# Latent attention: rotated query halves projected for eight heads at a time and passed through a DRAM scratch, both rotations ahead of all scores

## The chip, the cores and the metric

One Trainium2 chip, one core. The metric is the device time of one execution in microseconds (us), of which lower is better. Below, TensorE is the matrix engine, VectorE, ScalarE and GpSimd are the three engines for elementwise work, and SyncE issues nearly all DMAs. In the profile they are PE, DVE, ACT, POOL and SP.

## The reference

Two decoder layers over 512 tokens of width 1024, all in f32. Layer 0 mixes tokens with multi-head latent attention, layer 1 with a sparse attention; each layer then attends to 256 memory tokens and runs a gated feed-forward network, and a LayerNorm follows every part. The change lies in layer 0's latent attention alone:

```python
h = x @ w_in                                   # 512 + 256 + 32 columns
q = rms_norm(c_q) @ w_uq                       # 16 heads x (64 plain + 32 rotary)
q = concat(q[:64], rope(q[64:], pos))          # x1*cos - x2*sin, x1*sin + x2*cos
kv = rms_norm(c_kv) @ w_ukv                    # 16 heads x (64 key + 64 value)
k = concat(k_nope, rope(k_rope, pos))          # one 32-wide rotary key for all heads
p = softmax(mask(q @ k.T / sqrt(96)))          # causal, 512 x 512 per head
out = concat_heads(p @ v) @ w_o
```

## The kernel before

Every f32 operand of a matmul is split in two fp32r tiles, a high part `h` and the rest `l` (`split`, L94: ScalarE casts, VectorE or, if asked, GpSimd subtracts). `mm3` (L115) then makes one product out of three matmuls, h*h, h*l and l*h. `chunk` (L103) loads 512 KB of weights into one of three `raw` buffers through SyncE's queue and splits them into `wh` and `wl`, of which there are five each.

Tokens are the moving side, 512 columns at once. After the compressed projections (L465 to L545) come, in the order of the program, sixteen heads in pairs. `mla_proj(h)` (L565) projects the query of one head: 128 rows of output, which are 64 plain and 32 rotary rows, and the 32 rotary rows again with their halves swapped. A table multiplies them (`T0` for an even head, `T1` for an odd one: ones on the plain rows, cosine and signed sine on the others, L584), and the result is split. The key tile `K8` holds 64 plain key rows and the rotated key twice, so the sum over 128 rows of the product makes both terms of the rotation. At an even head it also projects the keys of the pair (6 matmuls) and loads the next weights. `mla_scores(h)` (L589) makes four score tiles of 128 queries and their softmax; `mla_t` (L603) transposes the probabilities, `mla_pv` (L624) multiplies them with the values, and at every odd head normalises and splits the output of the pair; `mla_v` (L516) projects values five steps ahead. The loop at L655 has `mla_t(h)`, `mla_scores(h + 1)`, `mla_proj(h + 3)`, `mla_pv(h)` and `mla_v(h + 5)`.

In the same loop `bias_rows` (L258) writes, head by head, a table of layer 1 to DRAM. The address ranges of two neighbouring rows overlap, so that each is issued when the one before has landed.

A planner orders each engine's instructions at compile time from the order of the program, a model of durations, and the buffers that are free; on the chip each engine then runs its list strictly in order and waits on semaphores. PSUM has four banks for projections, transposes and products with V (tag a) and four for scores and values (tag b). There are 39 tiles of 128x512 (`t2`) for nearly all that moves.

Of the kernel before, what the change touches and what calls it, by code (L numbers as in the profile page):

```python
# [11 lines left out]
F32 = mybir.dt.float32  # L12
FR = mybir.dt.float32r
# [7 lines left out]
P = 128  # L21
# [26 lines left out]
def _constants():  # L48
    c = np.zeros((P, 8), np.float32)
    r = np.arange(P)  # L50
    c[:, 0] = np.array(INV_FREQ, np.float32)[r % 16]
    sw = (r >= 64) & (r % 32 < 16)
    c[sw, 0] *= -1.0
    c[:64, 1] = 0.25
    c[:64, 2] = np.pi / 2
    lo = np.array(BUCKET_LO, np.float32)
    hi = np.concatenate([lo[1:], [np.float32(3e38)]])
    lo[0] = -3e38
    c[:, 3] = lo[r % 32]
# [7 lines left out]
def tile_hybrid_mla_dsa_deepnorm_block(ctx: ExitStack, tc: tile.TileContext, A: dict, out: bass.AP):  # L67
# [360 lines left out]
    def trig():  # L428
        posf, ang, kk = t2(), t2(), t2()
        nc.vector.tensor_copy(posf, posi)  # L430
        nc.vector.tensor_scalar(ang, posf, cst[:, 0:1], None, op0=ALU.mult)
        two_pi = 2 * math.pi
        pieces = []
        rest = two_pi
        for _ in range(2):
            e = math.frexp(rest)[1]
            q = math.ldexp(math.floor(math.ldexp(rest, 11 - e)), e - 11)
            pieces.append(q)
            rest -= q
        pieces.append(rest)  # L440
        MAGIC = 1.5 * 2.0 ** 23
        for sh in (20, 10, 0):
            s = 2.0 ** sh
            if sh:
                nc.vector.tensor_scalar(kk, ang, 1.0 / (two_pi * s), MAGIC, op0=ALU.mult, op1=ALU.add)
            else:
                nc.vector.tensor_scalar(kk, ang, 1.0 / two_pi, cst[:, 1:2], op0=ALU.mult, op1=ALU.add)
                nc.vector.tensor_scalar(kk, kk, MAGIC, None, op0=ALU.add)
            nc.vector.tensor_scalar(kk, kk, MAGIC, None, op0=ALU.subtract)
            for q in pieces:  # L450
                nc.vector.scalar_tensor_tensor(ang, kk, -q * s, ang, op0=ALU.mult, op1=ALU.add)
            yield
        nc.vector.tensor_scalar(ang, ang, cst[:, 2:3], math.pi, op0=ALU.add, op1=ALU.min)
        nc.vector.tensor_scalar(ang, ang, -math.pi, None, op0=ALU.max)
        nc.scalar.activation(TK, ang, AF.Sin)
        nc.vector.tensor_copy(T0[64:96], TK[0:32])
        nc.scalar.copy(T0[96:128], TK[64:96])
        nc.vector.tensor_copy(T1[0:32], TK[0:32])
        nc.scalar.copy(T1[32:64], TK[64:96])
        yield  # L460

    TK, T0, T1 = t2(), t2(), t2()
    nc.gpsimd.memset(T0[0:64], 1.0)
    nc.gpsimd.memset(T1[64:128], 1.0)
    ps2 = [bank("b") for _ in range(NT)]  # L465
    for c in range(4):
        h, l = XT[c // 2]
# [78 lines left out]

    ka = t2()
    kb_ = t2()
    nc.vector.tensor_tensor(ka[0:64], pk[0:64], TK[0:64], op=ALU.mult)
    nc.vector.tensor_tensor(kb_[0:64], pk[64:128], TK[64:128], op=ALU.mult)  # L550
    nc.vector.tensor_tensor(ka[0:64], ka[0:64], kb_[0:64], op=ALU.add)
    K8 = [t8(), t8()]
    for i, k8 in enumerate(K8):
# [8 lines left out]

    OTs = []

    def mla_proj(h):  # L565
        pr, e = h // 2, h % 2
        if e == 0:
            wts["q"] = chunk(A["w_uq"][pr], (P, 4, 256), nc.gpsimd if pr > 1 else None)
            if pr % 4 == 0:
                wts["k"] = chunk(A["w_uk"][pr // 4], (P, 2, 512))  # L570
            wk = wts["k"]
            pkk = bank("a")
            c0 = P * (pr % 4)
            for k in range(2):
                mm3(pkk, (wk[0][:, k, c0:c0 + P], wk[1][:, k, c0:c0 + P]), (ckv[0][:, k], ckv[1][:, k]), k == 0, k == 1)
            k8 = K8[pr % 2]
            split(k8[0:64, 0], k8[0:64, 1], pkk[0:64])
            split(k8[64:128, 2], k8[64:128, 3], pkk[64:128])
        wq = wts["q"]
        pq = bank("a")  # L580
        for k in range(4):
            mm3(pq, (wq[0][:, k, P * e:P * e + P], wq[1][:, k, P * e:P * e + P]), (cq[0][:, k], cq[1][:, k]), k == 0, k == 3)
        tq = t2()
        nc.vector.tensor_tensor(tq, pq, (T0, T1)[e], op=ALU.mult)  # L584
        q = (t2(FR), t2(FR))
        split(q[0], q[1], tq)
        return q

    def mla_scores(h, q):  # L589
        e = h % 2  # L590
        k8 = K8[h // 2 % 2]
        s01 = t2()
        sx = Softmax([s01[:, 0:128], s01[:, 128:384], t2()[:, 0:384], t2()])
        for qt in range(NT):
            n = P * (qt + 1)
            N = max(n, 256)
            ps = bank("b")
            ts_ = slice(P * qt, P * qt + P)
            mm3(ps[:, :N], (q[0][:, ts_], q[1][:, ts_]), (k8[:, 2 * e, :N], k8[:, 2 * e + 1, :N]), True, True)
            sx.exp(qt, ps[:, :n], MSC, mask[:, 512 - n:512])  # L600
        return sx

# [21 lines left out]
    def mla_pv(h, PT):  # L624
# [12 lines left out]
        if e == 1:  # L637
            pr_ = bank("a")
            for qt in range(NT):
                nc.tensor.transpose(pr_[:, P * qt:P * qt + P], rb[:, qt].rearrange("p a b -> p (a b)"), ident)  # L640
            nc.vector.tensor_tensor(of, of, pr_, op=ALU.mult)
            if pr < 4:
                oh_, ol_ = OT8[0][:, pr], OT8[1][:, pr]
            else:
                oh_, ol_ = t2(FR), t2(FR)
            OTs.append((oh_, ol_))
            split(oh_, ol_, of)

# [454 lines left out]
def layout(inputs):  # L1103
# [15 lines left out]
    cols = []  # L1119
    for h in range(16):  # L1120
        nope, rope = uq[:, h, :64], uq[:, h, 64:]
        rs = [rope, rope[:, 16:], rope[:, :16]]
        cols += [nope] + rs if h % 2 == 0 else rs + [nope]
    uq = np.concatenate(cols, 1)
    f["w_uq"] = uq.reshape(4, P, 8, 256).transpose(2, 1, 0, 3).reshape(8, P, 1024)
# [40 lines left out]
```

## Time and profile before

| | us |
|---|---|
| median of 3 runs (lowest, highest) | 1559.26 (1556.68, 1560.79) |
| the profiled execution | 1561.3 |
| its span, first to last instruction | 1559.5 |

One execution was profiled on the chip; all numbers are microseconds unless marked ns. A matmul's recorded duration overlaps the next one's, so the pace of a row of matmuls is read from their starts. PEld is the load of weights into TensorE. The latent attention's heads lie between about 56 and 216 us of the span.

### The profile page before, as it was taken

To read this page: it belongs to the slowest core of one execution; us is meant where nothing else is said; L and a number is where in the kernel's file an instruction comes from. 1 tells how busy PE (TensorE), PEld (TensorE's weight loads), DVE (VectorE), ACT (ScalarE), POOL (GpSimd) and SP (SyncE) were. 2 spreads that over 40 slices of the span, in tenths; PEclk is the share of its full clock that TensorE was granted. 3 is DMA by queue.
4 is the path that set the end of the run, shared out by engine and by line. 5 is a ranking of instruction groups with operands and counts; after the bars stand their busy time and mean duration, and the time that the engine had idled before them with its cause. 6 is when DMAs were issued, how large, how long until landed. Compare 5 with 4: busy or idle time off the path is not lost.

```text
span 1559.5 us, 20796 instructions
## 1 busy us (share of the span) xinstructions
PE 1513.7 (97%) x7948; PEld 1290.8 (83%) x7948; DVE 998.4 (64%) x1706; ACT 659.1 (42%) x1182; POOL 306.8 (20%) x303
## 2 busy tenths in 40 slices
PE   8999999999999999999999789999999999999997
PEld 7788778988888888888788678889888888888886
DVE  5887868454746565654668968785448466556545
ACT  4676753343233333332246489434332333333230
POOL 1322101000132331400125522010001323324002
PEclk9999999999999999999999899999999999999999
DMA  6234323322323232223241236243223132322221
GB/s 219 71 103 115 131 87 122 124 93 95 122 96 107 79 120 90 100 88 110 80 149 68 88 122 236 72 143 111 95 95 134 70 122 72 118 95 95 95 95 54
DMA packets 51320, 166.79 MB, mean 107 GB/s; under 512 B 5300, under 2 KB 11748, under 8 KB 49172
## 3 DMA queue, kind: packets, MB, share of 16 engines
q1 hardware_dynamic: 50788, 164.41, 30.8%
q8 instruction: 62, 1.02, 0.3%
q10 hardware_dynamic: 432, 1.05, 0.2%
q14 instruction: 38, 0.31, 0.1%
HBM read 161.20 MB, written 9.47 MB: 109 GB/s over the span
## 4 chain that ended last, share of the span: by engine, by line
PE 78%; DMA 8%; DVE 7%; ACT 4%; issue 1%; POOL 1%; SPq 0%; POOLq 0%; ACTq 0%; DVEq 0%
PE ps L118 24%; PE ps L116 24%; PE ps L117 24%; DMA scr<-vscr 4%; DVE t L96 2%; DVE wl L96 1%; ACT wh L95 1%; DMA raw<-in_mla_o_dram 1%; ACT t L95 1%; ACT t L405 1%; PE ps L324 1%; DVE t L954 1%; POOL sm L267 1%; PE ps L1022 1%; DVE m L953 1%
## 5 line engine op out<-in xcount | busy, mean ns | idle before, releaser
L116 PE MATMUL ps<-t,wh 128*128 128x512 f32 (+1 forms) x1264 | 459.1, 363 | 3.5 <-DVE t L96 3.4
L117 PE MATMUL ps<-t,wh 128*128 128x512 f32 (+1 forms) x1264 | 458.2, 362 | 0.9 <-DVE t L96 0.9
L118 PE MATMUL ps<-t,wl 128*128 128x512 f32 (+1 forms) x1264 | 458.1, 362 | 0.0
L95 ACT CAST wh<-raw 128x1024 fp32r<-128x1024 f32 (+2 forms) x218 | 227.4, 1044 | 470.5 <-PE ps L117 163.3
L96 DVE TENSOR_TENSOR wl<-raw,wh 128x1024 fp32r<-128x1024 f32 (+2 forms) x202 | 260.9, 1293 | 227.7 <-ACT wh L95 225.9
L116 PE MATMUL ps<-wh,t 128*128 128x512 f32 (+2 forms) x838 | 304.9, 364 | 3.8 <-DVE t L96 1.5
L118 PE MATMUL ps<-wh,t 128*128 128x512 f32 (+2 forms) x838 | 303.1, 362 | 1.0 <-DVE t L96 1.0
L117 PE MATMUL ps<-wl,t 128*128 128x512 f32 (+2 forms) x838 | 302.0, 360 | 0.0
L116 PEld LDWEIGHTS ps<-t,wh 128*128 128x128 f32 x1264 | 238.6, 189 | 41.6 <-DVE t L96 5.2
L117 PEld LDWEIGHTS ps<-t,wh 128*128 128x128 f32 x1264 | 238.6, 189 | 37.9 <-DVE t L96 1.4
L118 PEld LDWEIGHTS ps<-t,wl 128*128 128x128 f32 x1264 | 238.6, 189 | 36.7
L116 PEld LDWEIGHTS ps<-wh,t 128*128 128x128 f32 x838 | 158.8, 189 | 27.5 <-ACT t L95 1.8
L118 PEld LDWEIGHTS ps<-wh,t 128*128 128x128 f32 x838 | 158.8, 190 | 24.7 <-DVE t L96 1.4
L117 PEld LDWEIGHTS ps<-wl,t 128*128 128x128 f32 x838 | 158.9, 190 | 23.0
L95 ACT CAST t<-ps 128x512 fp32r<-128x512 f32 (+2 forms) x241 | 118.5, 523 | 132.2 <-PE ps L324 87.6
L265 POOL TENSOR_SCALAR sm<-sm 128x1 f32<-128x1 f32 x32 | 19.5, 608 | 678.9 <-DVE sm L299 635.9
L96 DVE TENSOR_TENSOR t<-ps,t 128x512 fp32r<-128x512 f32 (+2 forms) x241 | 138.7, 603 | 20.4 <-ACT t L95 19.6
L95 ACT CAST wh<-t 128x1024 fp32r<-128x1024 f32 x56 | 58.9, 1052 | 141.6 <-PE ps L117 123.6
L96 DVE TENSOR_TENSOR wl<-t,wh 128x1024 fp32r<-128x1024 f32 x56 | 71.2, 1272 | 64.9 <-ACT wh L95 63.1
L832 DVE TENSOR_TENSOR t<-ps,t 128x512 f32<-128x512 f32 x44 | 30.4, 691 | 120.4 <-PE ps L118 120.4
L96 DVE TENSOR_TENSOR t<-t,t 128x512 fp32r<-128x512 f32 (+2 forms) x113 | 84.0, 746 | 24.3 <-ACT t L95 22.1
L95 ACT CAST t<-t 128x512 fp32r<-128x512 f32 (+3 forms) x137 | 70.5, 525 | 59.6 <-POOL t L766 33.5
(176 smaller groups left out, 1687.5 us busy)
## 6 DMA issues: line engine op xcount, KB each, us to landing
raw<-in_ffn_in_dram SPq DMA_DIRECT2D x88, 512.0 KB, 3.2
t<-in_ffn_dg_dram SPq DMA_DIRECT2D x16, 1024.0 KB, 5.0
raw<-in_xa_k_dram SPq DMA_DIRECT2D x16, 512.0 KB, 3.3
raw<-in_xa_v_dram SPq DMA_DIRECT2D x16, 512.0 KB, 3.8
raw<-in_xa_q_dram SPq DMA_DIRECT2D x16, 512.0 KB, 3.9
raw<-in_xa_o_dram SPq DMA_DIRECT2D x16, 512.0 KB, 3.2
raw<-in_ffn_dl_dram SPq DMA_DIRECT2D x12, 512.0 KB, 3.2
scr<-vscr SPq DMA_DIRECT2D x16, 319.5 KB, 4.2
```

Of the source, the lines that this page charges most:

```text
L95: nc.scalar.copy(h, src)
L96: (eng or nc.vector).tensor_tensor(l, src, h.bitcast(F32), op=ALU.subtract)
L116: nc.tensor.matmul(ps, st[0], mv[0], start=start, stop=False, skip_group_check=more)
L117: nc.tensor.matmul(ps, st[0], mv[1], start=False, stop=False, skip_group_check=more)
L118: nc.tensor.matmul(ps, st[1], mv[0], start=False, stop=stop, skip_group_check=more)
L265: nc.gpsimd.tensor_scalar(a, var, scale, eps, op0=ALU.mult, op1=ALU.add)
L267: nc.gpsimd.tensor_tensor(b, a, mhalf, op=ALU.pow)
L324: nc.tensor.transpose(pt[:, k], x_of(tt)[:, 512 * n + P * k:512 * n + P * k + P], ident)
L405: nc.scalar.activation(Sx, src, AF.Exp, bias=nb, scale=scale, accum_out=self.sm[:, i:i + 1])
L832: nc.vector.tensor_tensor(sg, pu, sg, op=ALU.mult)
L953: nc.vector.max(out=m8, in_=acc[:, :n])
L954: nc.vector.match_replace(out=acc[:, :n], in_to_replace=m8, in_values=acc[:, :n], imm_value=-3e38)
```

## The change

The columns of the query weights are put in another order: first the rotary columns, 128 first halves and 128 second halves for eight heads, twice, then the plain columns of two heads at a time. `mla_rope(o)` projects the rotary halves of eight heads, rotates them with four multiplications and one subtraction and addition, splits the two results, and writes the four tiles to a DRAM scratch `rsc`, which is laid out by group, head, and high and low halves. `mla_nope(pr)` projects the plain halves of a pair and splits them. For each head it makes one stationary tile: GpSimd copies the 64 plain high rows, and a DMA reads the head's 64 rotary rows (high and low) from the scratch into the other 64. A second tile, `zq`, holds the plain low rows and zeros; three such pairs are kept, and their zeros are written once. `mla_k(pr)` is the key projection by itself. The scores still take three matmuls, the third now with `zq`. The cosine and sine tables are whole tiles. The split of a pair's output goes from VectorE to GpSimd.

Both calls of `mla_rope`, two of `mla_k` and two of `mla_nope` stand ahead of the first scores. In the loop `mla_k` comes at odd heads and `mla_nope` at even ones.

```diff
+    rsc = dp.tile([2, 8, 4, 16, S], F32, name="rsc")
...
-        nc.scalar.activation(TK, ang, AF.Sin)
-        nc.vector.tensor_copy(T0[64:96], TK[0:32])
-        nc.scalar.copy(T0[96:128], TK[64:96])
-        nc.vector.tensor_copy(T1[0:32], TK[0:32])
-        nc.scalar.copy(T1[32:64], TK[64:96])
+        for e in range(2):
+            nc.scalar.activation(COS[64 * e:64 * e + 64], ang[0:64], AF.Sin)
+            nc.scalar.activation(SIN[64 * e:64 * e + 64], ang[64:128], AF.Sin)
...
-    def mla_proj(h):
-        pr, e = h // 2, h % 2
-        if e == 0:
-            wts["q"] = chunk(A["w_uq"][pr], (P, 4, 256), nc.gpsimd if pr > 1 else None)
...
-        for k in range(4):
-            mm3(pq, (wq[0][:, k, P * e:P * e + P], wq[1][:, k, P * e:P * e + P]), (cq[0][:, k], cq[1][:, k]), k == 0, k == 3)
-        tq = t2()
-        nc.vector.tensor_tensor(tq, pq, (T0, T1)[e], op=ALU.mult)
-        q = (t2(FR), t2(FR))
-        split(q[0], q[1], tq)
-        return q
+    def q_block(w, c0):
+        ps = bank("a")
+        for k in range(4):
+            mm3(ps, (w[0][:, k, c0:c0 + P], w[1][:, k, c0:c0 + P]), (cq[0][:, k], cq[1][:, k]), k == 0, k == 3)
+        return ps
+
+    def mla_rope(o, eng):
+        w = chunk(A["w_uq"][o], (P, 4, 256))
+        x1, x2 = q_block(w, 0), q_block(w, P)
+        r1, r2, t1, t2_ = t2(), t2(), t2(), t2()
+        nc.vector.tensor_tensor(r1, x1, COS, op=ALU.mult)
+        nc.vector.tensor_tensor(r2, x1, SIN, op=ALU.mult)
+        nc.vector.tensor_tensor(t1, x2, SIN, op=ALU.mult)
+        nc.vector.tensor_tensor(t2_, x2, COS, op=ALU.mult)
+        eng.tensor_tensor(r1, r1, t1, op=ALU.subtract)
+        eng.tensor_tensor(r2, r2, t2_, op=ALU.add)
+        for i, r_ in enumerate((r1, r2)):
+            h_, l_ = t2(FR), t2(FR)
+            split(h_, l_, r_, eng)
+            nc.sync.dma_start(rsc[o, :, i], h_.bitcast(F32))
+            nc.sync.dma_start(rsc[o, :, 2 + i], l_.bitcast(F32))
+
+    def mla_nope(pr):
+        if pr % 2 == 0:
+            wts["q"] = chunk(A["w_uq"][2 + pr // 2], (P, 4, 256), nc.gpsimd if pr else None)
+        ps = q_block(wts["q"], P * (pr % 2))
+        qh, ql = t2(FR), t2(FR)
+        split(qh, ql, ps)
+        qa, qz = [], zq[pr % 3]
+        for e in range(2):
+            q = t2(FR)
+            rows, other = slice(64 * e, 64 * e + 64), slice(64 - 64 * e, 128 - 64 * e)
+            nc.gpsimd.tensor_copy(q[rows], qh[rows].bitcast(F32))
+            nc.gpsimd.tensor_copy(qz[e][rows], ql[rows].bitcast(F32))
+            nc.sync.dma_start(q[other].bitcast(F32), rsc[pr // 4, (2 * pr + e) % 8].rearrange("s i t -> (s i) t"))
+            qa.append(q)
+        qs[pr] = qa, qz
...
-            mm3(ps[:, :N], (q[0][:, ts_], q[1][:, ts_]), (k8[:, 2 * e, :N], k8[:, 2 * e + 1, :N]), True, True)
+            nc.tensor.matmul(ps[:, :N], qa[e][:, ts_], k8[:, 2 * e, :N], start=True, stop=False)
+            nc.tensor.matmul(ps[:, :N], qa[e][:, ts_], k8[:, 2 * e + 1, :N], start=False, stop=False)
+            nc.tensor.matmul(ps[:, :N], qz[e][:, ts_], k8[:, 2 * e, :N], start=False, stop=True)
...
-            split(oh_, ol_, of)
+            split(oh_, ol_, of, nc.gpsimd)
...
-    qs = {0: mla_proj(0), 1: mla_proj(1)}
-    Ss = {0: mla_scores(0, qs[0])}
-    qs[2] = mla_proj(2)
+    mla_rope(0, nc.vector)
+    mla_k(0)
+    mla_nope(0)
+    mla_nope(1)
+    mla_k(1)
+    mla_rope(1, nc.gpsimd)
+    Ss = {0: mla_scores(0)}
     for h in range(16):
         PT = mla_t(h, Ss.pop(h))
         if h + 1 < 16:
-            Ss[h + 1] = mla_scores(h + 1, qs[h + 1])
-        if h + 3 < 16:
-            qs[h + 3] = mla_proj(h + 3)
+            Ss[h + 1] = mla_scores(h + 1)
+        if h % 2 and h // 2 + 2 < 8:
+            mla_k(h // 2 + 2)
+        if h % 2 == 0 and 1 < h // 2 + 1 < 8:
+            mla_nope(h // 2 + 1)
         mla_pv(h, PT)
```

## Rows read from the trace of the kernel before

**Rows 1.** The page: busy time of each engine, and two lines in 40 slices.
```profile
PE 1513.7 (97%) x7948; PEld 1290.8 (83%) x7948; DVE 998.4 (64%) x1706; ACT 659.1 (42%) x1182; POOL 306.8 (20%) x303
...
PE   8999999999999999999999789999999999999997
...
PEclk9999999999999999999999899999999999999999
```

**Rows 2.** Busy time by stretch: opening, loop over heads, end of the loop.
```profile
core 0: us, PE busy (x) PEld busy (x) DVE busy (x) ACT busy (x) POOL busy (x), PEclk, DMA share, GB/s
56.00:72.00 16.00, 14.74 (x72) 11.66 (x71) 13.41 (x24) 9.52 (x20) 7.21 (x4) 1.00 0.30 108
72.00:182.00 110.00, 105.63 (x618) 90.36 (x616) 90.55 (x229) 80.50 (x205) 20.59 (x40) 1.00 0.31 88
182.00:216.00 34.00, 28.48 (x169) 23.87 (x169) 25.20 (x63) 21.46 (x55) 2.72 (x12) 1.00 0.37 137
```

**Rows 3.** Timeline of TensorE in the opening: start, duration, instruction.
```profile
56.71 0.48 PE L116 MATMUL ps<-t,wh 128*128 128x512 f32 x1
...
60.31 0.39 PE L116 MATMUL ps<-t,wh 128*128 128x512 f32 x1
...
64.85 0.39 PE L116 MATMUL ps<-t,wh 128*128 128x512 f32 x1
65.31 0.38 PE L116 MATMUL ps<-t,t 128*128 128x256 f32 x1
...
71.74 0.71 PE L613 MATMUL ps<-ident,t 128*128 128x128 f32 x5
```

**Rows 4.** Groups by form, 56 to 216 us: busy us, mean ns | idle before.
```profile
L96 DVE TENSOR_TENSOR t<-t,t 128x512 fp32r<-128x512 f32 x23 | 19.8, 860 | 5.0 <-ACT t L95 4.9
...
L95 ACT CAST t<-t 128x512 fp32r<-128x512 f32 x23 | 14.2, 616 | 10.9 <-DVE t L584 7.5 <-DVE t L641 3.1 <-DVE sm L409 0.3
...
L96 DVE TENSOR_TENSOR t<-ps,t 128x512 fp32r<-128x512 f32 x17 | 11.6, 681 | 1.6 <-ACT t L95 1.6
...
L584 DVE TENSOR_TENSOR t<-ps,t 128x512 f32<-128x512 f32 x16 | 11.1, 691 | 9.3 <-PE ps L118 9.2
...
L96 DVE TENSOR_TENSOR wl<-raw,wh 128x1024 fp32r<-128x1024 f32 x7 | 8.6, 1221 | 4.6 <-ACT wh L95 4.6
```

**Rows 5.** GpSimd's groups, 0 to 216 us: split of weights, two copies of keys.
```profile
L96 POOL TENSOR_TENSOR wl<-raw,wh 128x1024 fp32r<-128x1024 f32 x6 | 14.4, 2405 | 30.8 <-ACT wh L95 21.0 <-PE ps L632 8.0 <-PE ps L118 1.4
...
L560 POOL CAST t<-t 64x1024 fp32r<-64x1024 f32 x1 | 1.5, 1548 | 5.0 <-DVE t L557 5.0
L561 POOL CAST t<-t 64x1024 fp32r<-64x1024 f32 x1 | 1.0, 1048 | 0.1
```

**Rows 6.** Timeline of GpSimd and VectorE in the opening.
```profile
55.80 2.40 POOL L96 TENSOR_TENSOR wl<-raw,wh 128x1024 fp32r<-128x1024 f32 x1 [1.40 <-PE ps L118]
...
56.69 2.05 DVE L549 TENSOR_TENSOR t<-t,t 64x512 f32<-64x512 f32 x1
...
59.71 0.69 DVE L550 TENSOR_TENSOR t<-t,t 64x512 f32<-64x512 f32 x1
...
63.92 0.69 DVE L584 TENSOR_TENSOR t<-ps,t 128x512 f32<-128x512 f32 x1
```

**Rows 7.** DMA issues of the whole span: count, size of each, median us to landing.
```profile
scr<-vscr SPq DMA_DIRECT2D x16, 319.5 KB, 4.2
...
out_dram<-t SPq DMA_DIRECT2D x6, 256.0 KB, 2.0
...
t<-scr SPq DMA_DIRECT2D x4, 256.0 KB, 3.9
```

**Rows 8.** SyncE's queue in the loop: start and duration of the issues.
```profile
84.21 21.00 SPq L260 DMA_DIRECT2D scr<-vscr  x6
105.26 0.58 SPq L106 DMA_DIRECT2D raw<-in_w_uq_dram  x1
109.44 0.49 SPq L260 DMA_DIRECT2D scr<-vscr  x1
```

**Rows 9.** What TensorE waited for at the end of the loop, 182 to 216 us.
```profile
PE ps L632 <- DVE t L96: 3.3, 2, 2.0
PE ps L116 <- DVE t L96: 2.2, 1, 2.2
```

More of the change, by code (lines that the diff above doesn't have):

```diff
@@ L51, in _constants @@
     c[:, 0] = np.array(INV_FREQ, np.float32)[r % 16]
-    sw = (r >= 64) & (r % 32 < 16)
-    c[sw, 0] *= -1.0
+    c[:, 5] = np.where(r % 32 < 16, -1.0, 1.0)
     c[:64, 1] = 0.25
@@ L454, in trig @@
         nc.vector.tensor_scalar(ang, ang, -math.pi, None, op0=ALU.max)
-        nc.scalar.activation(TK, ang, AF.Sin)
-        nc.vector.tensor_copy(T0[64:96], TK[0:32])
-        nc.scalar.copy(T0[96:128], TK[64:96])
-        nc.vector.tensor_copy(T1[0:32], TK[0:32])
-        nc.scalar.copy(T1[32:64], TK[64:96])
+        for e in range(2):
+            nc.scalar.activation(COS[64 * e:64 * e + 64], ang[0:64], AF.Sin)
+            nc.scalar.activation(SIN[64 * e:64 * e + 64], ang[64:128], AF.Sin)
         yield
-    TK, T0, T1 = t2(), t2(), t2()
-    nc.gpsimd.memset(T0[0:64], 1.0)
-    nc.gpsimd.memset(T1[64:128], 1.0)
+    COS, SIN = t2(), t2()
     ps2 = [bank("b") for _ in range(NT)]
@@ L548, in tile_hybrid_mla_dsa_deepnorm_block @@
     kb_ = t2()
-    nc.vector.tensor_tensor(ka[0:64], pk[0:64], TK[0:64], op=ALU.mult)
-    nc.vector.tensor_tensor(kb_[0:64], pk[64:128], TK[64:128], op=ALU.mult)
+    nc.vector.tensor_tensor(ka[0:64], pk[0:64], COS[0:64], op=ALU.mult)
+    nc.vector.scalar_tensor_tensor(kb_[0:64], pk[64:128], cst[64:128, 5:6], SIN[64:128], op0=ALU.mult, op1=ALU.mult)
     nc.vector.tensor_tensor(ka[0:64], ka[0:64], kb_[0:64], op=ALU.add)
@@ L563, in tile_hybrid_mla_dsa_deepnorm_block @@
     OTs = []
-    def mla_proj(h):
-        pr, e = h // 2, h % 2
-        if e == 0:
-            wts["q"] = chunk(A["w_uq"][pr], (P, 4, 256), nc.gpsimd if pr > 1 else None)
[L569 to L580, printed above, removed]
-        for k in range(4):
-            mm3(pq, (wq[0][:, k, P * e:P * e + P], wq[1][:, k, P * e:P * e + P]), (cq[0][:, k], cq[1][:, k]), k == 0, k == 3)
-        tq = t2()
-        nc.vector.tensor_tensor(tq, pq, (T0, T1)[e], op=ALU.mult)
-        q = (t2(FR), t2(FR))
-        split(q[0], q[1], tq)
-        return q
@@ L589, in mla_scores @@
-    def mla_scores(h, q):
+    def q_block(w, c0):
+        ps = bank("a")
+        for k in range(4):
+            mm3(ps, (w[0][:, k, c0:c0 + P], w[1][:, k, c0:c0 + P]), (cq[0][:, k], cq[1][:, k]), k == 0, k == 3)
[15 more added lines that the diff above has]
+            nc.sync.dma_start(rsc[o, :, 2 + i], l_.bitcast(F32))
@@ L590, in mla_scores, with mla_k @@
+    def mla_k(pr):
+        if pr % 4 == 0:
+            wts["k"] = chunk(A["w_uk"][pr // 4], (P, 2, 512))
+        wk = wts["k"]
+        pkk = bank("a")
+        c0 = P * (pr % 4)
+        for k in range(2):
+            mm3(pkk, (wk[0][:, k, c0:c0 + P], wk[1][:, k, c0:c0 + P]), (ckv[0][:, k], ckv[1][:, k]), k == 0, k == 1)
+        k8 = K8[pr % 2]
+        split(k8[0:64, 0], k8[0:64, 1], pkk[0:64])
+        split(k8[64:128, 2], k8[64:128, 3], pkk[64:128])
+    def mla_scores(h):
         e = h % 2
@@ L591, in mla_scores @@
         k8 = K8[h // 2 % 2]
+        qa, qz = qs[h // 2]
         s01 = t2()
@@ L651, in tile_hybrid_mla_dsa_deepnorm_block @@
     OT8 = (t8(), t8())
-    qs = {0: mla_proj(0), 1: mla_proj(1)}
-    Ss = {0: mla_scores(0, qs[0])}
-    qs[2] = mla_proj(2)
+    qs = {}
+    zq = [[t2(FR) for _ in range(2)] for _ in range(3)]
+    for z in zq:
+        for e in range(2):
+            nc.gpsimd.memset(z[e][64 - 64 * e:128 - 64 * e].bitcast(F32), 0.0)
+    mla_rope(0, nc.vector)
[5 more added lines that the diff above has]
+    Ss = {0: mla_scores(0)}
     for h in range(16):
@@ L1118, in layout @@
     uq = I["mla_w_uq"][0].reshape(512, 16, 96)
[L1119 to L1125, printed above, removed]
+    nope = uq[:, :, :64].reshape(512, 1024)
+    rope = uq[:, :, 64:].reshape(512, 2, 8, 2, 16).transpose(0, 1, 3, 2, 4).reshape(512, 512)
+    uq = np.concatenate([rope, nope], 1)
+    f["w_uq"] = uq.reshape(4, P, 6, 256).transpose(2, 1, 0, 3).reshape(6, P, 1024)
     ukv = I["mla_w_ukv"][0].reshape(256, 16, 128)
```

## The prediction

> **What bounds the kernel now.** I read the page first: TensorE is busy in 97% of the span and no slice of it falls far below that, and the granted clock stands at nine tenths or more in all but one of them, far behind the attention [rows 1]. So a change pays by the matmul time it takes away, less the new waits it gives TensorE. Then the table by stage. The latent attention lasts from about 56 to 216 us. In its opening TensorE idles 16.00 - 14.74 = 1.3 us, in the loop over heads 110.00 - 105.63 = 4.4 us, at the end of the loop 34.00 - 28.48 = 5.5 us [rows 2]. VectorE is busy for 129.2 of these 160 us, ScalarE for 111.5, GpSimd for 30.5; all but the last could become the next bound. Third, the timeline of TensorE in the opening: the query projection of the first heads starts at 56.71, the first scores at 65.31, the first transposes of probabilities at 71.74 [rows 3]. Last, the rows that price single operations [rows 4, 5], and the DMA queue of SyncE [rows 7, 8].
>
> **TensorE.** A head's query projection is 4 x 3 = 12 matmuls of 512 columns, 16 heads 192. After the change two rotations take 2 x 24 and eight pairs of unrotated halves 8 x 12: 144. So 48 matmuls go. Their pace is not their own duration (they overlap): from 60.31 to 64.85 stand 20 steps, 4.54 / 20 = 0.227 us each [rows 3]. 48 x 0.227 = **10.9 us less**. The key projection, scores, transposes, values and everything behind the attention keep their matmuls. As TensorE is the busiest engine in the stage, I count this fully, and look for what is given back.
>
> **VectorE.** Away go 16 multiplications by the rotation table (0.69 each, 11.1 us), the 16 splits of their results and 8 splits of the head outputs, which move to GpSimd (24 x 0.86 = 20.6). New are 8 multiplications from PSUM in the rotations (5.5), 8 splits of the unrotated halves from PSUM (8 x 0.68 = 5.4), four SBUF operations of the first rotation (4 x 0.86 = 3.4) and one more weight split on VectorE (1.2) [rows 4]. Net about -16 us of 129: some 113 in about 152 us. ScalarE loses 16 casts of 0.62 and gets 12 of that size, and two weight chunks fewer. Neither becomes the bound; per head (thirteen in the 110 us) TensorE goes from 8.5 to 8.5 - 96 x 0.227 / 15 = 7.0 us, with VectorE near 7.0 - 1.2 = 5.8 and ScalarE near 6.2 - 0.3 = 5.9. These reliefs I count at nothing, since TensorE hides both now; if it didn't, they would only help.
>
> **GpSimd.** It loses three weight splits (3 x 2.4 = 7.2 us) and gets 32 copies of 64x512, half of the copies of twice that width, so 0.52 to 0.77 us each, 17 to 25 in all; four operations of the second rotation and 8 splits of head outputs, 128x512 at half of 2.4: 12 x 1.2 = 14.4 [rows 5]. That is +24 to +32 us, 55 to 62 of about 150: no bound by its sum. It is now in the path of the scores, though: projection (12 x 0.227 = 2.7), cast and split (0.6 + 0.7), then two copies before the first head of the pair can run (1.0 to 1.5), about 5.3 us, where the code gives one head, 7.0 us, since the unrotated half for pair p is written behind the scores of the head two before it. Cost between 0 (the program is laid out so that independent work moves ahead) and 2 us a pair when a head-output split and a copy of sums stand before it on GpSimd. Six pairs are built in the loop, so the ends are -1 (VectorE's relief shortens the loop's idle) and +12; I take +1, near the low end, because the trace's loop loses only 4.4 us in 13 heads with as many hand-overs.
>
> **The scratch round trip in the opening.** Before the first scores TensorE now has 24 (rotation), 6 (keys), 12, 12, 6 and 24 (second rotation) = 84 matmuls where it had 36: 48 x 0.227 = 10.9 us more, so the scores start at about 65.3 + 10.9 = 76.2 at the earliest. (The same 48 and another 48 are then missing in the loop: the 10.9 net.) VectorE is full until it reaches its first query operation at 63.92 [rows 6]. From there the first rotation takes 8 operations of 0.69, to 69.4. Then the write must land and the read behind it: 256 KB to DRAM took 2.0 us, and 256 KB back from the bias scratch 3.9 [rows 7]; for the 128 KB read I take 2.0 to 3.9, and 0.4 to issue. If the four writes fly together, the queries are complete between 73.8 and 75.7: hidden, with half a microsecond to spare at the worse end. If they are held one behind another, as the sixteen bias rows are (each is issued when the last has landed, 4.2 us apart [rows 8]), then from the first half at about 68.0 it is 4 x 2.0 + 0.4 + 2.0 to 3.9, that is 78.4 to 80.3, or up to 4.1 us late, 5.7 with writes slowed by the eight bulk reads in flight. Low end 0 (nothing in it speeds up TensorE), high end 5.7; I take **+1**, nearer to the low one, since writes to separate places are seen landing in 2.0 us and the bias rows, whose address ranges overlap, are no proof that these wait.
>
> Behind the first scores stood 18 matmuls of the third head's projection, 4.1 us, in which the softmax ran; now the program has none there. The next scores (12 matmuls, 67.87 less 65.31 in the old order, about 2.2 us) can fill, and the softmax behind the last score has to give about 1.5 us more: 0 to 2, I take **+1**. The second rotation costs VectorE 4 x 0.69 ahead of these scores, and its four writes stand in SyncE's queue until GpSimd is through (4 x 1.2 us); behind them wait only the bias table and weights for later pairs. They are covered by the eight heads before the second scratch is read, and cost nothing; if that cover went, the 2.0 + 3.9 of one round trip.
>
> **DMA in the loop.** Twelve reads of 128 KB go into the SyncE queue among the 16 bias rows. A read depends on the scratch alone, so it can be issued pairs ahead. I take 0; the other end is the third rival. At the end of the loop (5.5 us of idle, of which 3.3 before the product with V [rows 9]) the last three heads had no projection before and have none after; splits of the output go to GpSimd, where the last of them is covered by the output projection of seven other blocks. 0, with -2 to +3 as the ends.
>
> **Sum**: -10.9 + 1 + 1 + 1 = **-7.9 us** against the profiled execution (1559.5 span, 1561.3 with what lies around it), so 1553.4 for such an execution. The median of the runs, 1559.26, is 2.0 below it; from that, **1551**.
>
> **A rule to weigh.** While GpSimd split a weight (from 55.80 for 2.40 us), VectorE's product of two SBUF tiles took 2.05 us, the next of its kind 0.69 [rows 6]. The Trainium skill, "SBUF — State Buffer", section "Who interferes with whom", says that a VectorE operation with two SBUF inputs and a GpSimd operation that reads SBUF shut each other out for a whole instruction, and the trace agrees with these 2.05 us. As a mechanism of this kernel: the first rotation's four SBUF operations meet the two key copies on GpSimd (1.55 + 1.05 us), so the round trip starts 2.6 us later, which takes its spare half and leaves about 2.1 us; elsewhere 24 such pairs of operands leave VectorE, so nothing is added. That makes 1553, inside the forecast's own range.
>
> **Rivals.**
> (1) Everything is hidden: no wait is added, and VectorE's relief gives back about 2 of the loop's 4.4 us of idle. -10.9 - 2: 1546 to 1547. For it: 0.5 us to spare in the round trip, and -16 us on VectorE; against: less matmul work lies beside the same softmax.
> (2) The gain is eaten in the opening and by GpSimd: writes one by one (+5.7), the shut-out of 2.6, +1 behind the first scores: -1.6, 1558. For it: the bias rows do go one by one; against: 84 matmuls of cover.
> (3) Slower: the query reads stand in SyncE's queue behind bias rows that each wait for the one before. The chain of rows lasts 66 us now, nine of the new heads, five pairs. Five waits of one row, 5 x 4.2 = 21: -7.9 + 21 = +13, 1572. It decides from (7.9 + 4.7) / 5 = 2.5 us a pair on. For it: the weight loads at 105.26 and behind were issued only just after a row [rows 8]; against: TensorE's whole idle time in the loop, with all sixteen rows in it, is 4.4 us [rows 2].
>
> **Chances.** A difference under 0.3% (4.7 us) is what a measurement can't tell from none: faster is below 1554.6, slower above 1563.9. Forecast 0.45 (own range 1548 to 1556; 0.05 of it within 0.3%), rival 1 0.17, rival 2 0.20, rival 3 0.18. So faster 0.40 + 0.17 = 0.57, same 0.05 + 0.19 = 0.24, slower 0.18 + 0.01 = 0.19. The range takes rivals 1 and 2 and the near part of 3: 1546 to 1565.
>
> **What would show it.** In the changed profile: about 48 matmuls fewer, the first scores near 76, the last product with V some 8 us earlier; SyncE's four writes of the first rotation issued together, not 2 us apart; the idle of TensorE before its first scores under 2 us, and no group of waits of the scores on a DMA or a GpSimd copy that repeats with each pair. It is wrong if such a group sums to over 5 us, if VectorE or ScalarE comes over 85% in the loop, or if the matmuls' pace is not 0.227.

## The result and the profile after

| | before | after |
|---|---|---|
| median of 4 runs, us (lowest, highest) | 1559.67 (1556.68, 1560.79) | 1579.78 (1578.89, 1582.5) |
| ratio, 95% interval | | 1.0135 [1.0116, 1.0154] |
| span of the profiled execution, us | 1559.5 | 1580.3 |

The kernel became 20 us slower where the forecast was 8 us faster, and the time lies outside the range. The page of the kernel after, to be read beside [rows 1]:

```profile
span 1580.3 us, 20799 instructions
PE 1518.4 (96%) x7900; PEld 1294.7 (82%) x7900; DVE 985.9 (62%) x1685; ACT 655.6 (41%) x1177; POOL 340.1 (22%) x348
PEclk9998999999999999999999989999999999999999
```

The 48 matmuls are gone (7948 to 7900), and yet TensorE is busy for 4.7 us longer. VectorE and ScalarE have less to do, GpSimd has 33 us more. The stretches of [rows 2] (busy time and count of each engine, granted clock, DMA share, GB/s), the loop cut at 94 us, and the last one taken 22.8 us later, since the last product with V starts at 236.21 instead of 213.45:

```profile
56.00:72.00 16.00, 15.32 (x62) 12.59 (x61) 12.56 (x17) 5.55 (x10) 7.11 (x8) 0.79 0.24 89
72.00:82.00 10.00, 8.64 (x37) 6.49 (x35) 9.05 (x15) 5.60 (x9) 6.30 (x9) 1.00 0.63 201
82.00:94.00 12.00, 7.25 (x34) 6.55 (x34) 4.75 (x12) 6.47 (x15) 6.14 (x7) 0.72 0.54 170
94.00:182.00 88.00, 71.23 (x383) 60.20 (x384) 51.28 (x148) 52.01 (x142) 22.61 (x42) 0.88 0.34 93
204.80:238.80 34.00, 30.37 (x169) 24.98 (x168) 24.04 (x67) 22.60 (x60) 7.86 (x18) 0.95 0.40 146
```

In the loop TensorE now idles 88.00 - 71.23 = 16.8 us, where it idled 4.4 in 110, and no elementwise engine is over 60%. So it is a wait and not a busy engine. The waits of TensorE from 40 to 240 us (total, times, longest) name it; [rows 9] has no wait on a DMA:

```profile
PE ps L623 <- DMA t<-rsc: 20.5, 4, 5.9
PE ps L115 <- DVE t L95: 6.1, 5, 2.1
PE ps L625 <- POOL t L595: 0.5, 1, 0.5
```

Four times the scores wait for a read of the scratch: ahead of head 0, and of heads 4, 6 and 8. For GpSimd's copies they wait 0.5 us in all. SyncE's queue in the loop shows what the reads (L596) wait for; it answers [rows 8], a line that counts several issues gives the start of the first and the time to the end of the last, and loads that stand between are left out (`...`):

```profile
101.55 13.46 SPq L260 DMA_DIRECT2D scr<-vscr  x4
115.52 1.12 SPq L596 DMA_DIRECT2D t<-rsc  x2
118.78 0.53 SPq L260 DMA_DIRECT2D scr<-vscr  x1
...
123.82 9.19 SPq L260 DMA_DIRECT2D scr<-vscr  x3
...
137.03 0.49 SPq L260 DMA_DIRECT2D scr<-vscr  x1
137.62 1.89 SPq L596 DMA_DIRECT2D t<-rsc  x2
141.51 0.52 SPq L260 DMA_DIRECT2D scr<-vscr  x1
...
146.54 17.07 SPq L260 DMA_DIRECT2D scr<-vscr  x5
163.70 1.19 SPq L596 DMA_DIRECT2D t<-rsc  x2
```

The sixteen bias rows still go one by one; the first is issued at 101.55, the last at 167.62, 66.1 / 15 = 4.4 us each. Between the reads of heads 4 and 5 and those of heads 6 and 7 stand five rows, then six up to those of heads 8 and 9. The queue is in order, so each read is issued right behind a row that waited for its predecessor: the pair of heads can't come faster than 5 x 4.4 = 22 and 6 x 4.4 = 26 us. The first scores of heads 2, 4, 6 and 8 start at 97.91, 119.36, 142.18 and 168.21: 21.5, 22.8 and 26.0 us a pair. The rows set the pace.

The timeline of TensorE has the other two losses, the wait in the opening and the clock:

```profile
80.26 0.39 PE L117 MATMUL ps<-t,wl 128*128 128x512 f32 x1
85.71 0.55 PE L623 MATMUL ps<-t,t 128*128 128x256 f32 x1 [5.06 <-DMA t<-rsc]
...
119.36 0.55 PE L623 MATMUL ps<-t,t 128*128 128x256 f32 x1 [4.34 <-DMA t<-rsc]
...
122.16 0.63 PE L624 MATMUL ps<-t,t 128*128 128x512 f32 x1
122.58 0.63 PE L625 MATMUL ps<-t,t 128*128 128x512 f32 x1
```

and its stretch there:

```profile
121.00:124.00 3.00, 3.00 (x9) 2.52 (x9) 1.70 (x6) 0.86 (x4) 0.00 (x0) 0.50 0.83 215
```

The first scores start at 85.71, not at 76; and behind a wait the step of a 512-column matmul is 122.58 - 122.16 = 0.42 us, not 0.227: the granted clock is 0.50 there, the lower of its two levels, 1.2 GHz. It stands at 0.72 from 82 to 94 us and at 0.88 over the loop (both 1.00 in [rows 2] for the loop before).

### The profile page after: what moved, and what is told of

Same layout as the page of the kernel before. It is cut to its first block, busy times and chain, and to the rows that moved or that the text cites. A ratio compares the mean times of both kernels' runs of the same rounds, so it can differ in the third digit from the quotient of the medians.

```text
span 1580.3 us, 20799 instructions
## 1 busy us (share of the span) xinstructions
PE 1518.4 (96%) x7900; PEld 1294.7 (82%) x7900; DVE 985.9 (62%) x1685; ACT 655.6 (41%) x1177; POOL 340.1 (22%) x348
## 4 chain that ended last, share of the span: by engine, by line
PE 80%; DVE 7%; DMA 6%; ACT 3%; issue 2%; POOL 1%; SPq 0%; POOLq 0%; ACTq 0%; DVEq 0%
PE ps L115 24%; PE ps L117 24%; PE ps L116 24%; DMA scr<-vscr 4%; DVE t L95 1%; DVE wl L95 1%; ACT t L94 1%; ACT t L405 1%; PE ps L324 1%; DVE t L991 1%; POOL sm L267 1%; DVE sm L295 1%; PE ps L1059 1%; ACT wh L94 1%; DVE m L990 1%
## 5 line engine op out<-in xcount | busy, mean ns | idle before, releaser
L95 DVE TENSOR_TENSOR wl<-raw,wh 128x1024 fp32r<-128x1024 f32 (+1 forms) x203 | 263.2, 1299 | 228.2 <-ACT wh L94 226.6
L94 ACT CAST t<-ps 128x512 fp32r<-128x512 f32 (+4 forms) x249 | 122.5, 526 | 140.9 <-PE ps L324 87.8
L116 PEld LDWEIGHTS ps<-wl,t 128*128 128x128 f32 x838 | 159.3, 190 | 22.8
L95 DVE TENSOR_TENSOR t<-ps,t 128x512 fp32r<-128x512 f32 (+4 forms) x249 | 144.1, 607 | 42.2 <-ACT t L94 41.4
L95 DVE TENSOR_TENSOR wl<-t,wh 128x1024 fp32r<-128x1024 f32 x56 | 71.2, 1272 | 64.6 <-ACT wh L94 62.8
L94 ACT CAST t<-t 128x512 fp32r<-128x512 f32 (+2 forms) x125 | 63.1, 517 | 58.0 <-POOL t L803 33.5
L405 ACT ACTIVATE t<-t,sm 128x128 f32<-128x128 f32 (+3 forms) x128 | 71.3, 559 | 36.4 <-DVE sm L399 35.9
## 6 DMA issues: line engine op xcount, KB each, us to landing
scr<-vscr SPq DMA_DIRECT2D x16, 319.5 KB, 5.0
```

Source lines behind the costliest of these rows:

```text
L94: nc.scalar.copy(h, src)
L95: (eng or nc.vector).tensor_tensor(l, src, h.bitcast(F32), op=ALU.subtract)
L116: nc.tensor.matmul(ps, st[0], mv[1], start=False, stop=False, skip_group_check=more)
L405: nc.scalar.activation(Sx, src, AF.Exp, bias=nb, scale=scale, accum_out=self.sm[:, i:i + 1])
```

## The experiments

The chips differ (the median of the kernel before lay between 1559.7 and 1565.8 us on them), so kernels are compared by their ratio to the kernel before on the same chip. One thousandth is 1.56 us.

| run | ratio to the kernel before, 95% |
|---|---|
| after | 1.0135 [1.0116, 1.0154] |
| e_rows | 1.0101 [1.0078, 1.0124] |
| e_act | 1.0072 [1.0052, 1.0092] |
| e_lead | 1.0105 [1.0086, 1.0125] |
| e_dve | 1.0123 [1.0104, 1.0142] |
| b_ffn | 0.997 [0.9958, 0.9982] |
| r_ffn | 0.9962 [0.995, 0.9975] |
| r_split | 0.9961 [0.9949, 0.9973] |
| clk | 1.0122 [1.0106, 1.0138] |
| r_wide | 0.9948 [0.9936, 0.9961] |
| r_nort | 0.9942 [0.9928, 0.9956] |
| r_pre | 0.9968 [0.9955, 0.998] |
| r_best2 | 0.996 [0.9947, 0.9974] |

**The rows, moved behind the loop.**

```diff
-            bias_rows(h - 1)        # one row in each step of the loop
...
+    table = bias_table()            # behind the loop
+    next(table); next(table)
+    for h in range(16):
+        bias_rows(h)
```

> The bias table and its sixteen rows are moved behind the loop over heads; all else as changed. Theory A (the query reads stand in SyncE's queue behind bias rows that each wait for the one before): the three waits for the scratch in the loop (4.34, 5.17, 5.93 us) fall under 1 us each, with them the half-speed stretches of TensorE behind them (2.5 + 3.0 + 2.0 us of matmul time), so about -23 us: 1557, the wait of 5.06 us ahead of the first scores stays. Theory B (the tile that takes the read gets a free buffer too late, one head ahead): each wait shrinks by 1 us at most, 1575. If the rows cost as much behind the loop as in it, the three waits vanish but the time stays above 1570.

The three waits of the loop are gone, and the attention ends some 20 us earlier than in the kernel after: its first load of the next part's weights is issued at 223.8 instead of 244.4. Only a third of a per cent came out of it: the expectation's last case, waits gone and the time above 1570. The timeline of TensorE shows where it is given back:

```profile
280.30 0.58 PE L115 MATMUL ps<-t,wh 128*128 128x256 f32 x1 [9.98 <-ACT wh L94]
```

ScalarE, whose cast it waits for, had itself waited 21.7 us for weights of the next part, whose load was issued at 273.31, right behind a row. Another wait of 7.0 us at 301 follows behind ScalarE. So the queue's order, not the row's place in the loop, is what costs.

**The reads on ScalarE's queue; the reads a head earlier.**

```diff
-            nc.sync.dma_start(q[other].bitcast(F32), rsc[...])
+            nc.scalar.dma_start(q[other].bitcast(F32), rsc[...])   # e_act
...
-        if h % 2 == 0 and 1 < h // 2 + 1 < 8:
-            mla_nope(h // 2 + 1)
+        if h % 2 and h // 2 + 2 < 8:                                # e_lead
+            mla_nope(h // 2 + 2)
```

> The sixteen query reads are issued by ScalarE's DMA queue, the bias rows stay in SyncE's. Theory A: the three waits in the loop fall under 2 us each, 1557 to 1562, unless the reads hold up casts and exponentials on ScalarE. Theory B: the waits stay near 4 us, since the buffers come free no earlier, 1575 or more.

> The plain query halves of a pair, with their reads, are placed one head earlier in the program (two heads ahead of their scores, as the projection before was). Theory A: a read may still stand behind a row, but a row is 4.1 to 5 us and one head is 7 us, so the three waits in the loop go: 1557. Theory B: more lead does not free buffers, the planner leaves the reads where they are, within 5 us of 1580.

Both shortened the waits for the scratch (20.5 to 10.7 and 10.9 us), and both got a new one, which the waits of ScalarE from 100 to 200 us show; the first line is of e_act:

```profile
ACT wh L94 <- DMA raw<-in_mla_o_dram: 11.9, 1, 11.9
```

and this one of e_lead:

```profile
ACT wh L94 <- DMA raw<-in_mla_o_dram: 10.9, 1, 10.9
```

The output projection's weights stand behind rows too. Their cast blocks ScalarE, the casts of the probabilities stand behind it, and TensorE's product with V waits 8.7 and 10.6 us. Whatever is taken out of the rows' way, the next transfer in the queue is in it.

**The weight splits of the unrotated halves on VectorE instead of GpSimd.**

```diff
-            wts["q"] = chunk(A["w_uq"][2 + pr // 2], (P, 4, 256), nc.gpsimd if pr else None)
+            wts["q"] = chunk(A["w_uq"][2 + pr // 2], (P, 4, 256))
```

> The weight splits of the plain halves stay on VectorE (not GpSimd). The first rotation's subtraction, 2.74 us beside a GpSimd split of 2.39, falls to 0.69, so the writes to the scratch start 2 us earlier. If the opening's wait of 5.06 us hangs on that chain, it falls to about 3 and the time by 2 to 4 us, to 1576 to 1578; if it hangs on the writes landing (9.3 us from the last issue but one to the read), nothing moves. The loop's three waits stay.

The subtraction took 0.68 us, as expected:

```profile
66.89 0.68 DVE L576 TENSOR_TENSOR t<-t,t 128x512 f32<-128x512 f32 x1
```

The wait in the opening fell by 1.0 us, to 4.05. The kernel after is not the best partner here, since its granted clock is 0.57 from 56 to 64 us and that of e_dve 1.00. r_ffn (below) has the GpSimd split and, like e_dve, 1.00 there. From the same point (55.0 us) its first write is issued at 70.21 instead of 68.25 and its first scores start at 83.42 instead of 81.91. So the split on GpSimd holds some 1.5 us of the opening, and most of the wait is something else. SyncE's list came out another way as well: a weight load stands ahead of the fourth write, and six rows, not five, between the reads of heads 4 and 5 and those of heads 6 and 7. The waits of the loop grew (4.7, 8.8 and 8.0 us), and its pairs come 28.6 and 27.2 us apart, which is again the pace of six rows.

**The rows in the feed-forward network, with its control.** Each row now follows a weight load there, so that no load should stand behind more than one row.

```diff
                             w = chunk(A["ffn_in"][i, jj, gu], (P, NK, P))
+                            if todo_rows:
+                                with tc.issue_after(newest[0].ins):
+                                    bias_rows(todo_rows.pop(0))
```

> The kernel before with the 16 bias rows moved behind the latent attention and its output projection, into the feed-forward network of layer 0, each issued right behind one of its weight loads. It is the control for r_ffn: what the rows' place costs the kernel without the change. Theory A (the rows delay only what stands behind them in SyncE's queue, in the changed kernel the query reads): in the kernel before nothing on the path stands behind them but weights, so the time stays within 3 us, ratio 0.998 to 1.002. Theory B (the rows' packets slow every kernel by the load they put on the DMA engines, 16 MB-size transfers in the loop): it gets faster by some 5 us or more, ratio below 0.997.

> The changed kernel with the same move of the 16 bias rows into the feed-forward network of layer 0, each behind a weight load there, so that none stands ahead of a query read or a weight of the attention. Theory A (SyncE's order): the three waits of the scores in the loop (4.3, 5.2, 5.9 us) and the half-speed stretches behind them go, and unlike with all rows in one block behind the loop no weights come late later: 20 us less than the changed kernel, ratio to the kernel before 0.999 to 1.003; the opening wait of 4 to 5 us stays. Rival (the round trip itself or GpSimd's copies are late): waits of 2 us and more stay in the loop, ratio over 1.007.

The loop's waits are gone and are not given back later. TensorE's waits in r_ffn from 40 to 240 us:

```profile
PE ps L118 <- DVE t L95: 6.2, 5, 2.7
PE ps L626 <- DMA t<-rsc: 4.9, 1, 4.9
PE ps L626 <- POOL t L647: 1.0, 1, 1.0
```

and the first scores of heads 2, 4 and 6 in its timeline:

```profile
95.54 0.36 PE L626 MATMUL ps<-t,t 128*128 128x256 f32 x1
112.41 0.35 PE L626 MATMUL ps<-t,t 128*128 128x256 f32 x1
128.22 0.36 PE L626 MATMUL ps<-t,t 128*128 128x256 f32 x1
```

Head 8 follows at 144.97. From head 2 to head 8 it takes 49.4 us, the kernel after 70.3: 20.9 us, and the profiled spans differ by 1580.3 - 1556.9 = 23.4, of which 2.4 were there before head 2. By the ratios the rows' place costs the changed kernel (1.0135 - 0.9962) x 1560 = 27 us. In the control it costs the kernel before 0.3%, 4.7 us, more than the expectation's theory A; whether this is the weights behind the rows or the packets (a row has 319.5 KB [rows 7], not megabytes) was not separated. And b_ffn beside r_ffn is the change without the rows: 0.8 thousandths between them, the interval of each some 1.2 to either side. What the 48 matmuls bring can't be told from nothing there.

**The opening: writes cut in two.**

```diff
-            nc.sync.dma_start(rsc[o, :, i], h_.bitcast(F32))
+        for s0, s1 in ((0, 2), (2, 8)):          # heads 0 and 1, then the rest
+            ...
+                    nc.sync.dma_start(rsc[o, s0:s1, j], t_[16 * s0:16 * s1].bitcast(F32))
```

> r_ffn, and the four writes of each rotation are each cut in two: heads 0 and 1 first (four writes of 64 KB), then heads 2 to 7 (four of 192 KB), so the reads of the first pair depend on 256 KB instead of 1 MB. Theory (the opening wait is the time that 1 MB of writes takes on the DMA engines, beside the weight loads): the wait ahead of the first scores falls from 4 to 5 us to 0 to 2 us and the half-speed stretch behind it goes, some 5 us less than r_ffn, ratio to the kernel before 0.995 to 1.000. Rival (a fixed latency of a write and a read behind it): the wait stays within 1 us of r_ffn's, or grows by the four more issues (2 us).

The wait did not fall, it grew. TensorE in r_split, ahead of the first scores:

```profile
82.92 0.55 PE L630 MATMUL ps<-t,t 128*128 128x256 f32 x1 [6.49 <-DMA t<-rsc]
```

Its first read is issued at 77.84, 6.6 us behind the last of the four writes of 64 KB that it needs (issued by 71.2, its last completion event at 76.49). So 256 KB took longer than the 2.0 us of [rows 7]. The completion events in the trace suggest why: a load of 128 rows ends with sixteen, a write of the scratch in the kernel after with eight, those of r_split with two and six (besides one early event, some 1.1 us behind the issue). That is the number of heads, the outermost dimension of the write. The Trainium skill, "DMA: Bandwidth & Descriptors", section "Why a DMA increments its semaphore by 16 and not by 1", has the rule: a transfer runs on the largest number of engines, up to 16, that divides the outermost dimension of both its sides. The trace agrees with it in these counts (8; 2 and 6). That the count makes the write slow is what the next run tests.

**The scratch laid out as the tiles are.**

```diff
-    rsc = dp.tile([2, 8, 4, 16, S], F32, name="rsc")
+    rsc = dp.tile([2, 4, P, S], F32, name="rsc")
...
-            nc.sync.dma_start(rsc[o, :, i], h_.bitcast(F32))
+            nc.sync.dma_start(rsc[o, i], h_.bitcast(F32))
```

> r_ffn with the scratch laid out as the tiles are: each of the four results of a rotation is 128 rows of 2 KB one behind another, where the changed kernel has 8 heads x 16 rows, and a read gathers 4 blocks of 16 rows. In r_ffn and r_split a write of the scratch ends with as many completion events as it has heads (8, or 2 and 6), other transfers with 16, so I suspect that each write runs on 8 (2, 6) of the 16 DMA engines. Theory: the writes then run on 16 engines and 1 MB lands some 3 us earlier, the wait ahead of the first scores falls from 4.9 to about 2 us, 3 to 6 us less than r_ffn, ratio to the kernel before 0.992 to 0.995. Rival 1 (the writes are slow by their number of bytes or a fixed latency): the wait stays within 1 us of 4.9 and the time within 2 us of r_ffn. Rival 2: the reads, now 4 blocks, run on 4 engines and give 1 to 2 us back.

The writes came as expected, and so did the second rival. SyncE's queue in the opening of the kernel after, with the first write at 72.33 and the first read 10.8 us later:

```profile
72.33 1.39 SPq L581 DMA_DIRECT2D rsc<-t  x2
73.82 2.37 SPq L582 DMA_DIRECT2D rsc<-t  x2
76.66 0.98 SPq L105 DMA_DIRECT2D raw<-in_w_uq_dram  x1
83.15 2.43 SPq L596 DMA_DIRECT2D t<-rsc  x4
```

In r_wide the read comes 5.2 us behind the first write:

```profile
68.31 0.93 SPq L584 DMA_DIRECT2D rsc<-t  x2
69.45 0.92 SPq L585 DMA_DIRECT2D rsc<-t  x2
72.64 0.33 SPq L108 DMA_DIRECT2D raw<-in_w_uq_dram  x1
73.51 2.44 SPq L599 DMA_DIRECT2D t<-rsc  x4
```

Its timeline of TensorE has the wait:

```profile
78.66 0.36 PE L626 MATMUL ps<-t,t 128*128 128x256 f32 x1 [2.03 <-DMA t<-rsc]
```

Its fourth write, issued at 70.06, has sixteen completion events, the last at 73.49, 3.4 us later; in the kernel after the fourth, issued at 74.50, has the last at 83.13, 8.6 us later. The reads, now four blocks, end with four (and an early one): the first is issued at 73.51 and ends at 78.52, 5.0 us, where the first of r_ffn, with sixteen, goes from 80.78 to 83.29, 2.5 us. So this layout gains on the writes and gives 2.5 us back on the read that the first scores wait for. The wait fell from 4.90 (r_ffn) to 2.03; a second one of 1.3 us, ahead of head 6, is new. The time is 1.4 thousandths below r_ffn, with intervals that overlap: the profile shows the gain, the time alone would not.

**No round trip, and more cover.** In r_nort the first two pairs read a block that was written at the start. In r_pre the third pair's projections stand ahead of the first scores.

```diff
-            nc.sync.dma_start(q[other].bitcast(F32), rsc[...])
+            nc.sync.dma_start(q[other].bitcast(F32), dsc if pr < 2 else rsc[...])   # r_nort
...
     mla_k(1)
+    mla_nope(2)                                                                     # r_pre
+    mla_k(2)
```

> r_ffn in which the four reads of the first two pairs take a block of DRAM that is written at the start of the kernel, so they do not depend on the rotation (the scores of heads 0 to 3 are those of other numbers); the writes of the scratch stay. It prices the whole round trip of the opening. Theory (the opening's wait of 4.9 us and the 6.8 us of half clock behind it, some 2.5 to 3, are what keeps r_ffn from the forecast): first scores directly behind the matmuls ahead of them, 7 to 8 us less than r_ffn, ratio to the kernel before 0.990 to 0.993. Rival (VectorE and GpSimd, the casts and copies, are as late as the reads): a wait of 2 us and more on VectorE or GpSimd takes its place, ratio 0.994 to 0.997.

> r_ffn with the unrotated halves and the keys of the third pair (12 + 6 matmuls, 18 x 0.227 = 4.1 us) moved from the loop ahead of the first scores, as cover for the round trip. Theory: the wait ahead of the first scores falls from 4.9 to about 1 us and the half clock behind it goes; 4 to 6 us less than r_ffn, ratio 0.992 to 0.994. Rival (their casts and splits on VectorE and ScalarE and the copies on GpSimd delay the rotation or the first softmax, and heads 1 to 3 then have less work beside their softmax): the wait moves to the heads behind, the time within 2 us of r_ffn, ratio 0.995 to 0.998.

In r_pre the keys of the third pair overwrite those of the first ahead of its scores, so the scores of heads 0 and 1 are those of other numbers. r_nort is no faster than r_wide beyond the intervals; its scores still wait 1.6 us for the reads, which stand behind the writes in the queue, so it doesn't price the whole round trip. In r_pre the first scores wait 1.6 us, for a cast of ScalarE and no longer for a read, and its time can't be told from that of r_ffn: the rival. From the first scores to the last product with V it takes 125.6 us, only 2.3 less than r_ffn, although 18 matmuls (4.1 us) have left that stretch.

**Work in place of the waits, for the clock.**

```diff
+        nd = {0: 22, 4: 20, 6: 20, 8: 20}.get(h, 0)
+        if nd:
+            pd = bank("b")
+            for _ in range(nd):
+                nc.tensor.matmul(pd, qz[e][:, 0:P], k8[:, 2 * e], start=True, stop=True)
```

> The changed kernel with 82 matmuls of 128 stationary columns whose result nobody reads, put right ahead of the four groups of scores that wait for a query read (22 ahead of head 0, 20 each ahead of heads 4, 6 and 8): TensorE works where it idled. Theory (an idle stretch of 4 to 6 us is followed by 6.8 us at half the clock, which costs some 2.5 to 3 us a time): the reads land as late as before, the half-speed stretches go, and the kernel is 7 to 10 us faster than the changed one, ratio to the kernel before 1.007 to 1.009. Rival (half speed there has another cause, or costs nothing because the loop waits anyway): no gain, ratio 1.013, or slower by up to the 82 matmuls, 82 x 0.227 = 18.6 us, ratio up to 1.025.

In the opening it did what it was built for:

```profile
82.81 1.52 PE L622 MATMUL ps<-t,t 128*128 128x512 f32 x6
84.17 0.28 PE L628 MATMUL ps<-t,t 128*128 128x256 f32 x1
```

No wait, no half clock behind it. The scores of head 0, twelve matmuls, run from 84.17 to 86.11, 1.9 us, where the kernel after needs from 85.71 to 89.36, 3.65: half the clock costs 1.7 us in that head. But the time can't be told from that of the kernel after, so the expected 7 to 10 us were wrong. In the loop the waits moved (one of 6.0 and one of 7.3 us stayed), and the first scores of heads 2, 4, 6 and 8 lie 22.7, 28.3 and 27.0 us apart. The reads of heads 4, 6 and 8 are issued at 112.95, 139.74 and 167.04, with six rows between them each time, where the kernel after has five and then six. So the pairs still come at the pace of the rows, and the sixth row (some 4.4 us) takes away what the opening gained (head 2 at 94.24, 3.7 us ahead of the kernel after). What half the clock costs in the loop beside the rows is therefore not shown.

**A candidate.** r_wide, with each write cut in heads 0 and 1 and the rest, and two of the Sin activations later.

> A candidate that uses what the others showed: r_wide (rows in the feed-forward network, scratch laid out as the tiles are), the four writes of a rotation each cut in heads 0 and 1 (32 rows) and the rest (96 rows), and two of the four Sin activations put behind the last of the normalised compressed queries, since TensorE idles 2.1 us at the first key product behind ScalarE, where the kernel before has 1.5. Theory: the wait ahead of the first scores falls from 2.0 to under 1 us and the idle at 53 us to 1.5, 2 to 4 us less than r_wide, ratio to the kernel before 0.992 to 0.994. Rival (four more writes hold SyncE's queue 2 to 3 us longer, as in r_split, and VectorE is as late as the reads): the wait stays at 2 us or grows, ratio 0.994 to 0.997.

The wait for the scratch is 0.3 us (another of 1.1, for a cast, comes at head 1), but the idle of 2.1 us at 53 us stayed, and the ratio doesn't differ from r_wide's. That idle stands ahead of a product for the values (`mla_v`), not for the keys. r_wide and r_best2 are both faster than the kernel before, by 0.5% and 0.4%, each with an interval clear of 1. Beside b_ffn, the kernel before with its rows moved, r_wide has 2.2 thousandths, 3.4 us, with 1.8 thousandths of uncertainty: that is what the change is worth with the rows out of its way and the quicker writes.

## Why the prediction was wrong, step by step

- **DMA in the loop: the step that failed.** It said "A read depends on the scratch alone, so it can be issued pairs ahead. I take 0". What a read depends on was right, and in r_ffn those of head 8 are issued at 130.65, 14 us ahead of their use. But in the kernel after the order of SyncE's list puts the reads of heads 6 and 8 behind five and six rows that each wait for the one before. In place of 0 this cost 20.9 us from head 2 to head 8.
- **The third rival was the mechanism**, and its 21 us fit by chance of sizes: not five waits of one row, but three pairs, each as long as the rows between its reads. Its counter-argument, the 4.4 us of idle with all rows in the loop, misled me: behind a row stood only loads of weights for later then [rows 8]. An idle time measured before a change says nothing of a queue on whose path the change puts new work.
- **The round trip: mis-sized.** It was +1, with 5.7 as the end. Measured: a wait of 5.06 us, and half the clock behind it, 1.7 us in the first head. The writes were issued together, as forecast; the failed term is "256 KB to DRAM took 2.0 us" [rows 7], a price of writes of 128 rows, taken for one that is cut in 8 heads x 16 rows. Of four in flight the last took 8.6 us, and 3.4 with 128 rows (r_wide).
- **A count: "where it had 36".** It had 30, two projections of 12 and one product of 6 for the keys. So 54 matmuls come ahead of the first scores, 12.3 us, not 10.9, and the earliest start is 77.6, not 76.2; 102 leave the loop, not 96. The net of 48 stays.
- **The clock: left out.** The text asked for the pace of 0.227 and gave no price for half the clock behind a wait. In the opening it cost 1.7 us in the first head, and 2.4 us before it: from the value product that waits at 54.70 to the last matmul ahead of the scores at 80.26 the kernel after takes 25.6 us, with a granted clock of 0.50 from 57 to 62 us, and r_ffn 23.1 for the same matmuls, at 1.00.
- **A rule to weigh: it held, elsewhere.** The rotation's subtraction took 2.74 us beside a weight split of GpSimd; VectorE's timeline

```profile
68.31 0.68 DVE L575 TENSOR_TENSOR t<-ps,t 128x512 f32<-128x512 f32 x1
68.91 2.74 DVE L576 TENSOR_TENSOR t<-t,t 128x512 f32<-128x512 f32 x1
71.57 0.68 DVE L577 TENSOR_TENSOR t<-t,t 128x512 f32<-128x512 f32 x1
```

  and GpSimd's:

```profile
68.71 2.39 POOL L95 TENSOR_TENSOR wl<-raw,wh 128x1024 fp32r<-128x1024 f32 x1 [1.99 <-ACT wh L94]
```

  That is 2.1 us more ahead of the writes, near the 2.6 of the text, which expected the key copies as partner. Without the split (e_dve) it was 0.68.
- **Right:** 48 matmuls less; their pace at full clock; GpSimd no bound (0.5 us of waits for its copies); VectorE and ScalarE far below 85% in the loop (73 and 74% from the first scores on in r_wide, which the rows don't stretch); the end of the loop (idle 34.00 - 30.37 = 3.6 us after 5.5).
- **What is left of -10.9 us.** From the value product that waits in the opening (54.11 before, 53.23 in r_wide) to the last product with V it takes 159.3 us before and 154.9 in r_wide: -4.5, and -3.3 beside b_ffn (158.2), where the runs have -3.4 +- 2.8. The stretch from the first scores on, before:

```profile
65.31:213.45 148.14, 137.99 (x800) 117.34 (x801) 119.42 (x300) 106.62 (x269) 26.30 (x54) 1.00 0.33 100
```

  and in r_wide:

```profile
78.66:208.08 129.42, 120.32 (x700) 102.14 (x701) 94.44 (x265) 95.83 (x255) 46.15 (x85) 0.96 0.23 81
```

  Ahead of the first scores r_wide takes 25.4 us, 14.2 more than before, of which 12.3 are the 54 matmuls. Behind them its idle time is 1.1 us less, but it is busy only 17.7 us less where 102 matmuls at 0.227 are 23.2. The granted clock is 0.96 there and 1.00 before, so about 10 of the 129 us ran at half of it; by the steps of 0.42 and 0.227 that is some 5 us (an estimate). So most of what r_wide lacks goes with the clock; no run with the rows away restored the clock alone to show it.

## What to carry to other kernels

When a change puts a transfer on the path, write out the order of the queue that it is issued on: each item that waits for another transfer ahead of it is a delay, and a chain of them sets the pace for all that is behind. Price a DMA by the shape of its outermost dimension on both sides, the write and the read behind it (r_wide quickened one and slowed the other), and take a duration only from a row with the same shape. A time saved on the busiest engine is first tested on what it waits for next: here the same matmuls were worth nothing as long as the rows set the pace.

## What was not expected of the hardware

With four in flight, a 256 KB write of 128 rows to DRAM ended with sixteen completion events and the last took 3.4 us; of 8 blocks of 16 rows it ended with eight, and the last took 8.6 us. A read of 128 KB took 2.5 us with sixteen events and 5.0 with four. And half the clock does not follow each idle stretch alike: 2.13 us of idle at 54.70 were followed by it in the kernel after (0.79 from 56 to 72 us), 2.69 us at the same place in r_ffn were not (1.00 from 56 to 64). Why, no run here shows.
